# Prefix log-sum-exp along the sequence: later rows added in PSUM by VectorE in place of identity matmuls, and one drain of the chunk stream before the last tile

## Chip, cores and metric

One core of one Trainium2 chip. The metric is the device time of one execution in microseconds (us); a profiled execution has a span some 1.8 us below its time.

## The reference, cut to what matters

```python
B, S, D = (4, 4096, 4128)                     # x: float32, standard normal
out[:, 0, :] = x[:, 0, :]
for t in range(1, S):                          # running log-sum-exp over t
    out[:, t, :] = logaddexp(out[:, t - 1, :], x[:, t, :])
```

270.5 MB are read and 270.5 MB written.

## The kernel before

A tile holds up to 3 consecutive rows on each of 128 partitions, each row 4128 floats long: 6.34 MB. Each tile is worked off in four chunks of 1024 columns; the last chunk also carries a tail of 32 columns. ScalarE takes exp (as float16, written over the input), TensorE forms the prefix sum over the partitions into PSUM with triangular matrices, and ScalarE writes the logarithm of row 0. Row 1 is reached by adding its exps to PSUM with an identity matmul, then its logarithm is taken, then row 2. VectorE keeps the last partition's sum as a carry for the next tile.

```python
def stage(self, j):                            # row j of one chunk
    t, c, pt = self.t, self.c, self.pt
    nc.scalar.activation(t.xt[:, j, c * CH:(c + 1) * CH], pt, ACT.Ln)
    if j + 1 < t.r:
        for s in range(0, CH, MM):             # add row j + 1 by an identity matmul
            mm(pt[:, s:s + MM], ident, self.e(j + 1, s, s + MM), stop=j + 2 == t.r)
        if c == last and j == 0:               # the tail: 32 columns of all rows at once
            nc.scalar.activation(t.xt[:, :, t0:D], self.qt, ACT.Ln)
            keep(carry_t, self.qt[:, t.r - 1, :])
    else:
        keep(carry[c], pt)                     # two VectorE operations
...
chunks = [Chunk(s, c) for s in steps for c in range(n_main)]
for g in range(len(chunks) + R - 1):           # three chunks in flight, each one row apart
    for d in range(R - 1, -1, -1):
        if 0 <= g - d < len(chunks) and d < chunks[g - d].t.r:
            k = chunks[g - d]
            k.stage(d)
            if k.c == last and d + 1 == k.t.r:
                k.t.store()                    # then the load of the tile three ahead
                ...
    if g + 2 < len(chunks):
        chunks[g + 2].exp()
    if g + 1 < len(chunks):
        chunks[g + 1].head()
```

Four tile buffers, so three loads run ahead. Four of the 44 tiles have two rows: the first, and the last of the other three batches. T is the tile before the last, L the last. The matmuls with which a chunk begins are called its head below, and the two VectorE operations that save its carry its carry pair.

The softmax here doesn't subtract the row's maximum and nothing guards it: scores larger than these inputs give would overflow.

## Time and profile before

| | before |
|---|---|
| time, median | 1262.82 us |
| DMA | 541 MB, share 9 tenths or more in 39 of 40 slices |
| ScalarE / TensorE / VectorE busy | 75% / 55% / 36% |
| granted TensorE clock | 0.77 |

In a group line the number after the bar is busy time in us, then the mean in ns of one; after the second bar comes the idle time just before these instructions and what ended most of it.

### The profile page before, as it was taken

What the parts mean: (1) busy time and instruction counts of PE and PEld (TensorE: products, weight loads), DVE (VectorE), ACT (ScalarE), POOL (GpSimd) and SP (SyncE); (2) the same over time, 40 slices, a digit from 0 to 9 for tenths busy, and PEclk for the clock granted to TensorE, in tenths of its full rate; (3) what the DMA queues carried; (4) which work ended last, traced back from release to release, by engine and by line L of the source; (5) the groups of instructions that cost most, each with busy time, mean ns of one, the idle gap of its engine ahead of it and who ended that gap; (6) DMA issues with size and microseconds to landing.
All of it is one profiled execution on the core that took longest, in us unless ns stands there. A gap on an engine that the chain in (4) does not pass through costs nothing.

```text
span 1261.0 us, 6165 instructions
## 1 busy us (share of the span) xinstructions
PE 688.7 (55%) x2268; PEld 237.0 (19%) x2268; DVE 451.4 (36%) x445; ACT 947.3 (75%) x733; POOL 2.2 (0%) x13
## 2 busy tenths in 40 slices
PE   3665554555555555655346555555634755664552
PEld 1222111111121111211112211111211211221120
DVE  2443333333333333334424333333442433333344
ACT  5997777777777777778569777777966977777794
POOL 0000000000000000000000000000000000000000
PEclk9887777777677777777768777787777777778786
DMA  9999999999999999999999999999999999999998
GB/s 411 410 439 431 432 427 434 438 430 432 433 437 431 432 432 436 432 427 436 431 433 436 437 429 431 436 436 432 430 434 435 432 431 432 434 435 431 433 422 347
DMA packets 12702, 541.46 MB, mean 429 GB/s; under 512 B 1408, under 2 KB 1408, under 8 KB 1408
## 3 DMA queue, kind: packets, MB, share of 16 engines
q1 hardware_dynamic: 12672, 541.07, 99.4%
q8 instruction: 18, 0.29, 0.1%
q14 instruction: 12, 0.10, 0.0%
HBM read 270.53 MB, written 270.53 MB: 429 GB/s over the span
## 4 chain that ended last, share of the span: by engine, by line
DMA 69%; ACT 21%; PE 5%; issue 2%; DVE 1%; SPq 0%; ACTq 0%
DMA xt<-in_x_dram 67%; ACT xt L128 11%; ACT xt L162 10%; PE pt L88 5%; DMA out_dram<-xt 2%; ACT xt L167 0%; SPq L116 0%; DVE carry L92 0%; DVE carry L93 0%; ACTq L231 0%; SPq L113 0%; ACTq L128 0%; PE qt L88 0%
## 5 line engine op out<-in xcount | busy, mean ns | idle before, releaser
L128 ACT ACTIVATE xt<-xt 128x3072 f16<-128x3072 f32 (+3 forms) x176 | 478.5, 2719 | 247.9 <-DMA xt<-in_x_dram 247.8
L88 PE MATMUL pt<-xt,ident 128*128 128x512 f16 x672 | 251.3, 470 | 530.7 <-ACT xt L162 530.4
L162 ACT ACTIVATE xt<-pt 128x1024 f32<-128x1024 f32 x512 | 487.6, 1030 | 2.5 <-PE pt L88 0.7
L92 DVE CAST carry<-pt 32x1024 f16<-32x1024 f32 x176 | 216.4, 1230 | 761.0 <-ACT xt L162 760.7
L88 PE MATMUL pt<-xt,excl 128*128 128x512 f16 x672 | 247.0, 504 | 0.0
L93 DVE TENSOR_TENSOR carry<-pt,carry 32x1024 f16<-32x1024 f32 x176 | 215.9, 1227 | 6.1
L88 PEld LDWEIGHTS <-ident 128*128 128x128 f16 x672 | 70.1, 104 | 677.7 <-issue 654.0
L88 PE MATMUL pt<-xt,incl 128*128 128x512 f16 x352 | 152.0, 526 | 23.6 <-ACT xt L128 15.0
L88 PEld LDWEIGHTS <-excl 128*128 128x128 f16 x756 | 92.5, 124 | 141.0 <-issue 108.1
L88 PE MATMUL pt<-carry,pick 128*128 128x512 f16 x320 | 109.8, 429 | 0.0
L88 PEld LDWEIGHTS <-incl 128*128 128x128 f16 x480 | 45.2, 111 | 129.7 <-DVE carry L93 95.2
L88 PEld LDWEIGHTS <-pick 128*128 128x128 f16 x360 | 40.6, 113 | 57.0 <-issue 34.3
L167 ACT ACTIVATE xt<-qt 128x96 f32<-128x96 f32 (+1 forms) x44 | 10.9, 249 | 45.7 <-PE pt L88 45.7
L92 DVE CAST carry_t<-qt 32x32 f16<-32x32 f32 x44 | 8.7, 197 | 25.5 <-ACT xt L167 25.4
L88 PE MATMUL qt<-xt,incl 128*128 128x64 f16 (+2 forms) x128 | 12.3, 196 | 0.0
L88 PE MATMUL qt<-xt,excl 128*128 128x64 f16 (+1 forms) x84 | 10.6, 187 | 0.0
L93 DVE TENSOR_TENSOR carry_t<-qt,carry_t 32x32 f16<-32x32 f32 x44 | 8.5, 193 | 1.5
L88 PE MATMUL qt<-carry_t,pick 128*128 128x96 f16 (+1 forms) x40 | 8.2, 204 | 0.0
L83 DVE MEMSET carry<- 128x512 uint32 x4 | 1.9, 485 | 1.1 <-PEq L220 1.0
L70 ACT ACT_TABLE_LOAD x1 | 1.3, 1283 | 0.8 <-PEq L220 0.8
L35 POOL TENSOR_SCALAR_AFFINE_SELECT pick<-pick 128x128 f16<-128x128 f16 x2 | 0.6, 294 | 0.1
L25 POOL TENSOR_SCALAR_AFFINE_SELECT incl<-incl 128x128 f16<-128x128 f16 x1 | 0.3, 294 | 0.0
(11 smaller groups left out, 1.9 us busy)
## 6 DMA issues: line engine op xcount, KB each, us to landing
xt<-in_x_dram SPq DMA_DIRECT2D x40, 6192.0 KB, 42.2
out_dram<-xt SPq DMA_DIRECT2D x40, 6192.0 KB, 28.1
xt<-in_x_dram SPq DMA_DIRECT2D x4, 4128.0 KB, 37.3
out_dram<-xt SPq DMA_DIRECT2D x4, 4128.0 KB, 23.0
```

The costliest lines, as they stand in the source:

```text
L25: nc.gpsimd.affine_select(out=t, in_=t, pattern=[[1, P]], compare_op=mybir.AluOpType.is_ge, fill=0.0, base=base, channel_multiplier=-1,)
L35: nc.gpsimd.affine_select(out=t, in_=t, pattern=[[step, P]], compare_op=mybir.AluOpType.not_equal, fill=1.0, base=base, channel_multiplier=1,)
L70: nc.scalar.preload_act_table_set("natural_log_exp_and_others")
L83: nc.vector.memset(t, 0.0)
L88: nc.tensor.matmul(pt, lhsT=w, rhs=rhs, start=start, stop=stop, skip_group_check=True)
L92: nc.vector.tensor_copy(cr[HI:HI + 32, :], pt[HI:HI + 32])
L93: nc.vector.tensor_tensor(out=cr[LO:LO + 32, :], in0=pt[HI:HI + 32], in1=cr[HI:HI + 32, :], op=mybir.AluOpType.subtract,)
L128: nc.scalar.activation(self.t.half[:, :, 2 * c0:2 * c0 + w], self.t.xt[:, :, c0:c0 + w], ACT.Exp,)
L162: nc.scalar.activation(t.xt[:, j, c * CH:(c + 1) * CH], pt, ACT.Ln)
L167: nc.scalar.activation(t.xt[:, :, t0:D], self.qt, ACT.Ln)
```

## The change

The intent: take load off TensorE and use a VectorE that is idle two thirds of the time; and let the next to last tile's store go out without waiting for the last tile's exps. For that the stream of chunks is drained: all chunks of T are finished before L's first exp. The diff is shortened; lines with `...` or in brackets stand for what is left out.

```diff
     def stage(self, j):
         nc.scalar.activation(t.xt[:, j, c * CH:(c + 1) * CH], pt, ACT.Ln)
         if j + 1 < t.r:
-            for s in range(0, CH, MM):
-                mm(pt[:, s:s + MM], ident, self.e(j + 1, s, s + MM), stop=j + 2 == t.r)
+            add(pt, pt, self.e(j + 1, 0, CH))            # VectorE, in place in PSUM
             if c == last and j == 0:
                 nc.scalar.activation(t.xt[:, :, t0:D], self.qt, ACT.Ln)
     def tail_head(self):
+        e = [self.e(i, CH, CH + tail) for i in range(r)]
         for i in range(r):                               # before: all rows by broadcast matmuls
-            e = self.e(i, CH, CH + tail)
-            mm(qt[:, i:, :], incl, to(e, r - i), start=i == 0)
-            if i:
-                mm(qt[:, :i, :], excl, to(e, i))
+            mm(qt[:, 0, :], excl if i else incl, e[i], start=i == 0)
...
+        for i in range(1, r):
+            add(qt[:, i, :], qt[:, i - 1, :], e[i])
...
-    chunks = [Chunk(s, c) for s in steps for c in range(n_main)]
-    (one stream of chunks)
+    for part in (steps[:-1], steps[-1:]):                # the stream drains in between
+        chunks = [Chunk(s, c) for s in part for c in range(n_main)]
+        (the same loop)
```

More of the change, by code (lines that the diff above doesn't have):

```diff
@@ L29, in tri, with ones_at @@
         return t
-    def ones_where_zero(bases, step, name):
+    def ones_at(rows, name):
         t = pool.tile([P, P], FP16, name=name)
         nc.gpsimd.memset(t, 0.0)
-        for base in bases:
+        for row in rows:
             nc.gpsimd.affine_select(
-                out=t, in_=t, pattern=[[step, P]], compare_op=mybir.AluOpType.not_equal,
-                fill=1.0, base=base, channel_multiplier=1,
+                out=t, in_=t, pattern=[[0, P]], compare_op=mybir.AluOpType.not_equal,
+                fill=1.0, base=-row, channel_multiplier=1,
             )
@@ L43, in _constants @@
         tri(-1, "excl"),
-        ones_where_zero([0], -1, "ident"),
-        ones_where_zero([-(HI + 31), -(LO + 31)], 0, "pick"),
+        ones_at([HI + 31, LO + 31], "pick"),
     )
@@ L71 @@
     consts = ctx.enter_context(tc.tile_pool(name="consts", bufs=1))
-    incl, excl, ident, pick = _constants(nc, consts)
+    incl, excl, pick = _constants(nc, consts)
     bufs = 4
@@ L85, with mm, add @@
     ctx.enter_context(tc.manual_schedule())
-    def mm(pt, w, rhs, start=False, stop=False):
-        nc.tensor.matmul(pt, lhsT=w, rhs=rhs, start=start, stop=stop, skip_group_check=True)
+    def mm(pt, w, rhs, start=False):
+        nc.tensor.matmul(pt, lhsT=w, rhs=rhs, start=start, stop=False, skip_group_check=True)
+    def add(o, a, v):
+        nc.vector.tensor_tensor(out=o, in0=a, in1=v, op=mybir.AluOpType.add)
     def keep(cr, pt):
@@ L149, in tail_head @@
             qt = self.qt = full[:, :r, :]
-            to = lambda v, n: v.unsqueeze(1).to_broadcast([P, n, tail])
+            e = [self.e(i, CH, CH + tail) for i in range(r)]
             for i in range(r):
-                e = self.e(i, CH, CH + tail)
-                mm(qt[:, i:, :], incl, to(e, r - i), start=i == 0)
-                if i:
-                    mm(qt[:, :i, :], excl, to(e, i))
+                mm(qt[:, 0, :], excl if i else incl, e[i], start=i == 0)
             if not t.first:
-                mm(qt, pick, to(carry_t, r))
+                mm(qt[:, 0, :], pick, carry_t)
+            for i in range(1, r):
+                add(qt[:, i, :], qt[:, i - 1, :], e[i])
         def stage(self, j):
@@ L188 @@
     stored = 0
-    chunks[0].exp()
-    chunks[1].exp()
-    chunks[0].head()
-    for g in range(len(chunks) + R - 1):
-        for d in range(R - 1, -1, -1):
-            if 0 <= g - d < len(chunks) and d < chunks[g - d].t.r:
+    for part in (steps[:-1], steps[-1:]):
+        chunks = [Chunk(s, c) for s in part for c in range(n_main)]
+        chunks[0].exp()
+        chunks[1].exp()
+        chunks[0].head()
+        for g in range(len(chunks) + R - 1):
+            for d in range(R - 1, -1, -1):
+                if not (0 <= g - d < len(chunks) and d < chunks[g - d].t.r):
+                    continue
                 k = chunks[g - d]
@@ L201 @@
                     stored += 1
-        if g + 2 < len(chunks):
-            chunks[g + 2].exp()
-        if g + 1 < len(chunks):
-            chunks[g + 1].head()
+            if g + 2 < len(chunks):
+                chunks[g + 2].exp()
+            if g + 1 < len(chunks):
+                chunks[g + 1].head()
 _INS = ['x']
```

## The prediction

> **What bounds the kernel now.** I read the page's engine totals and its forty slices first, then the groups, then the SyncE queue's waits, and last the end of the run in two-microsecond windows and in order of time, because the first views say that only the ends can matter.
>
> ```profile
> span 1261.0 us, 6165 instructions
> ...
> PE 688.7 (55%) x2268; PEld 237.0 (19%) x2268; DVE 451.4 (36%) x445; ACT 947.3 (75%) x733; POOL 2.2 (0%) x13
> ...
> DMA  9999999999999999999999999999999999999998
> ...
> q1 hardware_dynamic: 12672, 541.07, 99.4%
> ...
> L88 PE MATMUL pt<-xt,ident 128*128 128x512 f16 x672 | 251.3, 470 | 530.7 <-ACT xt L162 530.4
> L162 ACT ACTIVATE xt<-pt 128x1024 f32<-128x1024 f32 x512 | 487.6, 1030 | 2.5 <-PE pt L88 0.7
> L92 DVE CAST carry<-pt 32x1024 f16<-32x1024 f32 x176 | 216.4, 1230 | 761.0 <-ACT xt L162 760.7
> ...
> L93 DVE TENSOR_TENSOR carry<-pt,carry 32x1024 f16<-32x1024 f32 x176 | 215.9, 1227 | 6.1
> ```
>
> No compute engine is above 75%, while the DMA engines are at 9 tenths or more in 39 of 40 slices. 541.07 MB at the 433 GB/s or so of the middle slices is 1250 us of the 1261. One full tile (three rows of 4128 floats on 128 partitions, 6.34 MB) takes 14.6 us each way, and the stores are indeed issued 29.3 us apart (1153.25, 1182.61, 1212.01 in the SyncE queue). ScalarE needs only about 21.9 us per tile: four times one exp (2.66 from start to start) and three Ln (0.92 each), 5.4 us per chunk, plus 0.25. It then waits for the next load, 247.8 us in all. So in the stream a compute change is hidden as long as a store is issued before the transfers in the queue run out. A store takes 28.1 us to land against 14.6 of its own, so at each issue the slowest DMA engine still holds some 13.5 us of older work. Only the start, where the queue is short, and the end, where nothing is left to overlap, can show the change.
>
> The end, as windows (the last three fields are PE clock, DMA share, GB/s):
>
> ```profile
> 1226.00:1228.00 2.00, 1.54 (x7) 0.60 (x7) 0.51 (x3) 1.89 (x2) 0.00 (x0) 1.00 0.80 347
> 1228.00:1230.00 2.00, 0.00 (x0) 0.00 (x0) 0.90 (x1) 2.00 (x4) 0.00 (x0) 1.00 0.63 272
> 1230.00:1232.00 2.00, 1.64 (x5) 0.55 (x5) 1.56 (x2) 2.00 (x2) 0.00 (x0) 0.65 0.23 99
> 1232.00:1234.00 2.00, 2.00 (x6) 0.70 (x5) 0.36 (x1) 2.00 (x3) 0.00 (x0) 0.50 0.10 33
> 1234.00:1236.00 2.00, 0.85 (x4) 0.13 (x2) 1.97 (x2) 2.00 (x3) 0.00 (x0) 0.99 0.93 396
> ```
>
> and the same stretch in order of time (start, length, engine):
>
> ```profile
> 1220.78 1.91 ACT L128 ACTIVATE xt<-xt 128x2048 f16<-128x2048 f32 x1 [1.34 <-DMA xt<-in_x_dram]
> ...
> 1233.63 10.83 SPq L116 DMA_DIRECT2D out_dram<-xt  x2
> ...
> 1243.09 1.02 ACT L162 ACTIVATE xt<-pt 128x1024 f32<-128x1024 f32 x1
> ```
>
> Call the tile before the last T (three rows) and the last one L (two rows, 4.23 MB). L's load lands at 1220.7. The queue then runs dry: the shares of the four windows from 1226 to 1234 fall 4.5 us short of full. T's store comes only at 1233.6, because ScalarE runs L's first three exps between T's last Ln's. From 1234 T's 6.34 and L's 4.23 MB flow without a gap until 1258.2, and the span ends 2.8 us later. L's store is issued at 1244.1, while T's transfer lasts until 1234.0 + 14.6 = 1248.6: L has 4.5 us of slack today.
>
> **What the Trainium skill says.** "VectorE: DVE Perf Modes", section "The perf-mode tier table", gives tensor_tensor with any PSUM operand only the 1x mode; its errata section has (N+151)/0.96 ns for an fp32 add, 1224 ns at N = 1024. The trace agrees: the subtraction with a PSUM input and 1024 columns took 1227 ns. Partitions should not matter, so I take 1.23 us for the new 128x1024 add, and 1.27 from start to start as between the two carry operations (1229.10, 1230.37). "PSUM — Partial Sum Buffer", section "The four PSUM rules", says that VectorE's writes leave the accumulation bits alone; here no matmul follows an add in its group, so the result is safe. "DMA: Bandwidth & Descriptors", section "Where 436 GB/s comes from", puts the ceiling at 435.2 GB/s; the 427 to 439 of the middle slices agree, so the stream has nothing to gain.
>
> **The change, part by part.**
> (1) Removed: 672 identity matmuls, 251.3 us of PE and 70.1 us of weight loads; none on the DMA path. PE goes to about 430 us.
> (2) Added on VectorE: 336 adds of 1.23 us, 413 us, and 84 tail adds at about 0.2 (as the 32-column rows take 0.19 to 0.20), 17 us: 451 + 430 = 881 us, 70%. Per chunk it now has two carry operations and two adds, 4 x 1.27 = 5.1 us, against ScalarE's 5.4. It fits, barely, and the tail adds can push it over by a microsecond once per tile. With some 13.5 us of work queued that costs nothing in the stream. Under load ScalarE's Ln's find their operand ready; the 1.1 us that the tail's Ln waits for an identity matmul queued behind it is gone, so stores come 0.6 to 1.3 us earlier. At the start, where tile 1's store (63.44) meets an almost empty queue, that may save 0.3 us.
> (3) The drain. All of T must now leave before L's first exp, and while no exps are in between, VectorE (5.1 us per round of four operations) and not ScalarE sets the pace, since each Ln of a chunk waits for an add that stands behind another chunk's carry pair. I lay out the instructions in the changed program's order with the durations above. (The same laying-out of the kernel before gives 1233.65 and 1244.2 for its last two stores, against 1233.63 and 1244.1 measured.)
>
> T's load landing at 1196.2 as before, T's fourth exp starts at 1212.6 (before: 1213.65). T0's third, T1's second and T2's first Ln run from 1215.4 to 1218.2. VectorE: carry T0 1216.4 to 1218.9, add T1 to 1220.2, add T2 to 1221.5, tail adds to 1221.9. ScalarE waits: T1's third Ln at 1220.2, T2's second at 1221.5, T3's first at 1222.4, the tail's at 1223.3. VectorE: carry T1 1221.9 to 1224.4, add T2 to 1225.7, add T3 to 1227.0, tail carry and carry T2 to 1230.0, add T3 to 1231.2. T3's third Ln ends at 1232.3: T's store goes out 1.3 us earlier than before, no more.
>
> L then starts at 1232.2, where before its first exp ran at 1220.8. Exps L0 and L1 to 1235.9, L0's first Ln 1235.8, exp L2 1236.7, L0's second Ln 1238.5, L1's first 1239.4, exp L3 1240.3. VectorE: carry L0 1239.6 to 1242.1, add L1 to 1243.3; L1's second Ln 1243.4, L2's first 1244.3; carry L1 to 1246.9, add L2 to 1248.2; L2's second Ln 1248.2, L3's first 1249.1; carry L2 1249.3 to 1251.8, add L3 to 1253.1; L3's second Ln ends at 1254.1. L's store goes out 10 us later than before.
>
> (4) Sum. T's transfer runs 1232.8 to 1247.4; then the DMA stands idle until L's store at 1254.1 + 0.5 = 1254.6, where before it began at 1248.6. The end moves by 6.0 us. With 0.3 saved at the start and some 0.4 for eight to ten hand-overs between VectorE and ScalarE that I took at 0.03 each: 1262.87 + 6.0 - 0.3 + 0.4 = 1269.0.
>
> **Rivals.**
> (a) The drain pays: T's store fills the hole that opens at 1226, and L keeps up. The 4.5 us short in the windows is the most that it can give: 1258.5. For it speaks the intent; against it L's 4.5 us slack, which an 11.4 us later start of its first exp uses up.
> (b) VectorE becomes the bound of the stream. It would take adds above 1.4 us (two carry operations of 1.27 and two of those exceed 5.4), and then ScalarE, at 5.4 x 4 = 21.9 us of 29.3, would still have over 7 us to give. Speaking for it only the start, 27 to 64 us, where ScalarE is busy 28.3 of 30 us and the queue short: 1 to 3 us more, 1271.
> (c) The matmul clock: at half clock (0.50 and 0.65 in the windows at 1230 to 1234) a head of L takes 2.8 us instead of 1.5. My schedule has few places where it shows, T3's head and L0's first; about 2.4 us more, 1271.4. Against: fewer matmuls should leave the clock high, and it is 1.00 in most windows of the end.
> (d) L's instructions overlap better than laid out, and all moves are hidden: 1263.
>
> **Range and chances.** The direction rests on one fact of order (L's exps behind T's last Ln) and on durations that are measured. (c) and slow hand-overs give the upper end, 1273; shorter drains and part of (a) the lower, 1263.5. A change of 2% is 25 us, and T's and L's drains together are not that long, so within 2% is nearly sure: 0.97. Slower by over 2% would need the stream itself to lose its DMA bound: 0.02. Faster by over 2% is below the transfer time of 541 MB: 0.01.
>
> **What would show it.** The new add at 1.2 to 1.25 us; VectorE near 880 us and PE near 430; stores in the stream still 29.3 us apart. At the end: T's store 1 to 2 us before 1233.6, ScalarE idle several times for 1 to 2 us on VectorE's adds, L's first exp directly after T's last Ln, L's store near 1254, the DMA share at zero for about 6 us around 1250, and the span near 1267. I am wrong if L's store comes before 1249, or if the store spacing in the stream changes.

## More of the kernel before

The page is shown in the prediction. One more group of it, which the prediction did not show, turned out to matter, the tail's Ln of the kernel before:

```profile
L167 ACT ACTIVATE xt<-qt 128x96 f32<-128x96 f32 (+1 forms) x44 | 10.9, 249 | 45.7 <-PE pt L88 45.7
```

44 short Ln's, one per tile, each found ScalarE waiting, 1.04 us on average, for an identity matmul into `pt`. The Ln reads `qt`, not `pt`.

## The result, and the profile after

The changed kernel takes 1281.99 us (median; 1281.17 to 1282.36) against 1262.82 before. Ratio 1.0151, 95% interval 1.0133 to 1.0168. It is slower by 1.5%. Predicted were 1269.0, with a range of 1263.5 to 1273.

The page of the changed kernel, the lines that answer to those in the prediction:

```profile
span 1280.6 us, 5200 instructions
...
PE 544.8 (43%) x1512; PEld 176.2 (14%) x1512; DVE 865.4 (68%) x865; ACT 950.6 (74%) x733; POOL 1.8 (0%) x11
...
DMA  9989999999999999999999999999999999999986
...
L160 ACT ACTIVATE xt<-pt 128x1024 f32<-128x1024 f32 x512 | 490.8, 1027 | 20.0 <-DVE pt L89 17.2
...
L89 DVE TENSOR_TENSOR pt<-pt,xt 128x1024 f32<-128x1024 f32 x336 | 398.1, 1228 | 26.9 <-ACT xt L160 21.5
...
L164 ACT ACTIVATE xt<-qt 128x96 f32<-128x96 f32 (+1 forms) x44 | 10.9, 248 | 145.2 <-DVE pt L89 145.2
```

The add takes 1228 ns, as predicted, and VectorE's busy time (865 us, 881 predicted) is right. But the third of the DMA slices is at 8 tenths, so the stream's start lost transfers, and the tail's Ln now waits 145.2 us, 3.3 per tile, where it waited 1.04.

What one such wait looks like in order of time in the changed kernel (start, length, engine; in square brackets the engine's idle time before and what ended it; TensorE rows left out):

```profile
577.42 2.83 ACT L160 ACTIVATE xt<-pt 128x1024 f32<-128x1024 f32 x3
578.45 1.23 DVE L93 CAST carry<-pt 32x1024 f16<-32x1024 f32 x1 [2.73 <-ACT xt L160]
579.72 1.23 DVE L94 TENSOR_TENSOR carry<-pt,carry 32x1024 f16<-32x1024 f32 x1
580.98 2.36 DVE L89 TENSOR_TENSOR pt<-pt,xt 128x1024 f32<-128x1024 f32 x2
...
583.37 0.25 ACT L164 ACTIVATE xt<-qt 128x96 f32<-128x96 f32 x1 [3.12 <-DVE pt L89]
583.52 2.75 ACT L129 ACTIVATE xt<-xt 128x3072 f16<-128x3072 f32 x1
```

ScalarE is done with its three Ln's at 580.25. It then stands still until 583.37, until VectorE has finished a carry pair and two chunk adds, though the tail's own two adds were done before (they ran at 575.29). Only then can the next exp start.

Where this costs transfers, the start, in windows of five microseconds (after the length: busy us of TensorE, its weight loads, VectorE, ScalarE and GpSimd; the last three fields are granted clock, DMA share and GB/s). Before:

```profile
60.00:65.00 5.00, 4.45 (x12) 1.38 (x12) 2.06 (x3) 5.00 (x4) 0.00 (x0) 0.67 0.82 357
65.00:70.00 5.00, 2.50 (x11) 0.90 (x11) 1.87 (x2) 4.97 (x5) 0.00 (x0) 1.00 1.09 466
```

After:

```profile
60.00:65.00 5.00, 1.67 (x4) 0.29 (x2) 1.51 (x4) 4.57 (x4) 0.00 (x0) 0.50 1.10 476
65.00:70.00 5.00, 3.09 (x8) 1.02 (x8) 4.43 (x5) 5.00 (x5) 0.00 (x0) 0.53 0.00 0
```

The second tile's store is issued at 69.66 instead of 63.44, the third's at 96.28 instead of 86.17, and for five microseconds nothing moves at all. After the fourth store, and away from the two-row tiles at the batch boundaries, stores are some 29.3 us apart as before.

The end of the changed kernel, in order of time:

```profile
1239.43 0.25 ACT L164 ACTIVATE xt<-qt 128x96 f32<-128x96 f32 x1 [4.46 <-DVE pt L89]
...
1244.47 1.02 ACT L160 ACTIVATE xt<-pt 128x1024 f32<-128x1024 f32 x1 [2.96 <-DVE pt L89]
1245.39 3.84 ACT L129 ACTIVATE xt<-xt 128x2048 f16<-128x2048 f32 x2
...
1267.67 1.02 ACT L160 ACTIVATE xt<-pt 128x1024 f32<-128x1024 f32 x1
```

and in windows:

```profile
1242.00:1244.00 2.00, 0.00 (x0) 0.00 (x0) 1.97 (x2) 0.00 (x0) 0.00 (x0) 0.50 0.00 0
...
1260.00:1262.00 2.00, 0.00 (x0) 0.00 (x0) 1.94 (x3) 0.00 (x0) 0.00 (x0) 0.50 0.00 0
```

T's last Ln runs at 1244.47 and L's first exp directly behind it; T's store goes out at 1245.5, L's at 1268.7, against 1233.6 and 1244.1 before. Between 1260 and 1268 VectorE works, ScalarE mostly waits for it and the DMA stands idle.

### The profile page after: what moved, and what is told of

Read it like the earlier page. It is cut to its first block, busy times and chain, and to the rows that moved or that the text cites. A ratio compares the mean times of both kernels' runs of the same rounds, so it can differ in the third digit from the quotient of the medians.

```text
span 1280.6 us, 5200 instructions
## 1 busy us (share of the span) xinstructions
PE 544.8 (43%) x1512; PEld 176.2 (14%) x1512; DVE 865.4 (68%) x865; ACT 950.6 (74%) x733; POOL 1.8 (0%) x11
## 4 chain that ended last, share of the span: by engine, by line
DMA 58%; ACT 18%; DVE 16%; PE 6%; issue 1%; ACTq 0%; SPq 0%
DMA xt<-in_x_dram 58%; ACT xt L129 12%; ACT xt L160 6%; PE pt L86 6%; DVE carry L93 5%; DVE carry L94 5%; DVE pt L89 5%; ACT xt L164 1%; DVE qt L89 0%; ACTq L232 0%; PE qt L86 0%; SPq L114 0%; SPq L117 0%; ACTq L129 0%; ACTq L160 0%
## 5 line engine op out<-in xcount | busy, mean ns | idle before, releaser
L86 PE MATMUL pt<-xt,incl 128*128 128x512 f16 x352 | 161.1, 555 | 714.1 <-DVE carry L94 527.4
L93 DVE CAST carry<-pt 32x1024 f16<-32x1024 f32 x176 | 216.4, 1230 | 314.3 <-ACT xt L160 314.0
L89 DVE TENSOR_TENSOR pt<-pt,xt 128x1024 f32<-128x1024 f32 x336 | 398.1, 1228 | 26.9 <-ACT xt L160 21.5
L86 PE MATMUL pt<-xt,excl 128*128 128x512 f16 x672 | 295.0, 585 | 0.0
L94 DVE TENSOR_TENSOR carry<-pt,carry 32x1024 f16<-32x1024 f32 x176 | 215.8, 1226 | 6.1
L86 PE MATMUL pt<-carry,pick 128*128 128x512 f16 x320 | 151.2, 570 | 0.0
L86 PEld LDWEIGHTS <-incl 128*128 128x128 f16 x396 | 31.3, 107 | 828.9 <-issue 821.1
L164 ACT ACTIVATE xt<-qt 128x96 f32<-128x96 f32 (+1 forms) x44 | 10.9, 248 | 145.2 <-DVE pt L89 145.2
L86 PEld LDWEIGHTS <-pick 128*128 128x128 f16 x360 | 48.8, 136 | 80.4 <-issue 74.1
L89 DVE TENSOR_TENSOR qt<-qt,xt 128x32 f32<-128x32 f32 x84 | 16.7, 198 | 42.0 <-PE qt L86 40.6
L86 PE MATMUL qt<-xt,incl 128*128 128x32 f16 x44 | 9.3, 212 | 0.0
L86 PE MATMUL qt<-xt,excl 128*128 128x32 f16 x84 | 9.1, 183 | 0.0
L86 PE MATMUL qt<-carry_t,pick 128*128 128x32 f16 x40 | 7.3, 183 | 0.0
```

The source lines that it names most:

```text
L86: nc.tensor.matmul(pt, lhsT=w, rhs=rhs, start=start, stop=False, skip_group_check=True)
L89: nc.vector.tensor_tensor(out=o, in0=a, in1=v, op=mybir.AluOpType.add)
L93: nc.vector.tensor_copy(cr[HI:HI + 32, :], pt[HI:HI + 32])
L94: nc.vector.tensor_tensor(out=cr[LO:LO + 32, :], in0=pt[HI:HI + 32], in1=cr[HI:HI + 32, :], op=mybir.AluOpType.subtract,)
```

## The experiments

Theory W: the tail's Ln is one instruction over all rows. Its 32 columns lie at the end of each row, so as one stretch of addresses it runs from the end of row 0 to the end of row 2, and all the exps that the chunk adds of rows 1 and 2 still read lie inside. It is therefore held for these adds, with which it shares no element. In the kernel before the same hold fell on identity matmuls, which were quick; now it falls on VectorE's adds, which queue behind a carry pair. Rival V: it is VectorE's load and the low matmul clock that slow every round. Rival D: it is the drain. Whether the hold is put into the program when it is built or made by the chip, no run here shows; the profile infers what released a wait from semaphore events.

### The hold taken away

```diff
-  nc.scalar.activation(t.xt[:, :, t0:D], self.qt, ACT.Ln)
+  for i in range(t.r):
+      nc.scalar.activation(t.xt[:, i, t0:D], self.qt[:, i, :], ACT.Ln)
```

> The changed kernel with the Ln of the 32 tail columns written row by row (three small Ln's in place of one over all rows), nothing else moved. Theory W (a held wait): the one Ln over all rows spans, as a stretch of addresses, the rows that VectorE's chunk adds still read, so it is held until the adds of the last two chunks are done; ScalarE idles 3.3 us per tile for it, which empties the transfer queue at the start and lengthens the end. W expects the wait of the tail's Ln to fall from 145 us to under 40, the second tile's store at 62 to 64 us (not 69.7), no window without transfers at 65 to 70, and 1269 to 1272 us, near what was first predicted. Rival V (VectorE's load and the low matmul clock slow every round, the wait is incidental): second store still after 67, 1278 to 1282. Rival D (the drain is nearly all of the loss): 1278 to 1282 too.

Measured: 1270.26 us, ratio 1.0058 (1.0043 to 1.0073). Correct result. The group and one round:

```profile
L165 ACT ACTIVATE xt<-qt 128x32 f32<-128x32 f32 x128 | 16.5, 217 | 0.0
```

```profile
1198.59 2.83 ACT L160 ACTIVATE xt<-pt 128x1024 f32<-128x1024 f32 x3
1199.62 1.23 DVE L93 CAST carry<-pt 32x1024 f16<-32x1024 f32 x1 [6.72 <-ACT xt L160]
...
1201.30 0.38 ACT L165 ACTIVATE xt<-qt 128x32 f32<-128x32 f32 x3
...
1202.15 2.36 DVE L89 TENSOR_TENSOR pt<-pt,xt 128x1024 f32<-128x1024 f32 x2
```

The three small Ln's run at 1201.30, before VectorE's two adds at 1202.15, and the result is correct, so there is no data they need from them. The wait is 0.0. The second store is back at 63.55 (before: 63.44) and the window from 65 to 70 us has a DMA share of 1.09. 11.7 us of the 19.2 are gone. W holds; V and D each expected 1278 or more.

### The Ln moved ahead of the last chunk's add

```diff
-  add(pt, pt, self.e(j + 1, 0, CH))
   if c == last and j == 0:
       nc.scalar.activation(t.xt[:, :, t0:D], self.qt, ACT.Ln)
       keep(carry_t, self.qt[:, t.r - 1, :])
+  add(pt, pt, self.e(j + 1, 0, CH))
```

> The changed kernel with the tail's Ln (still one over all rows) and its carry issued ahead of the last chunk's first add. W in its exact form: the Ln is then held only by the add of the chunk before, which VectorE finishes 1.27 us earlier, so the wait falls by 1.2 to 1.4 us per tile, from 145 to about 90 us, the second store comes near 67, and the time is 1276 to 1279, between the changed kernel and e1. If the wait were for the tail's own adds or matmuls (rival), nothing changes: 1281 to 1282. If only the last chunk's add held it, all of it goes: 1269 to 1272.

Measured: 1274.54 us, ratio 1.0093.

```profile
L163 ACT ACTIVATE xt<-qt 128x96 f32<-128x96 f32 (+1 forms) x44 | 10.9, 248 | 86.0 <-DVE pt L89 86.0
```

```profile
576.12 1.23 DVE L89 TENSOR_TENSOR pt<-pt,xt 128x1024 f32<-128x1024 f32 x1
...
577.39 0.25 ACT L163 ACTIVATE xt<-qt 128x96 f32<-128x96 f32 x1 [1.99 <-DVE pt L89]
...
578.11 1.23 DVE L89 TENSOR_TENSOR pt<-pt,xt 128x1024 f32<-128x1024 f32 x1
```

The wait fell from 145.2 to 86.0, 1.35 us per tile: about one add's length, not to zero. The Ln starts when the add of the chunk before ends; the last chunk's own add now comes after it, at 578.11. So the Ln is held by the add of the chunk before as well, which reads other columns. That is what a stretch of addresses predicts and what neither the tail's own data nor the last chunk alone does. The time fell by more than I expected (1276 to 1279), probably because only what exceeds the queue's reserve (the transfers still queued when a store is issued) is lost: T's load landed at 1196.74 in this run, against 1204.23 in the changed kernel and 1195.92 without the hold. With two microseconds per tile held instead of three, nearly all the lost transfers were back.

### Each part alone

Adds and the held Ln without the drain (`for part in (steps,):`):

> The changed kernel with one chunk stream over all tiles, so without the drain. W: the start loses as before (second store near 69.7); laid out by hand with the corrected wait, the last two stores come near 1247.5 and 1265, and the time is 1278 to 1279.5: the drain was worth only 2 to 3 us. D (the drain is nearly all of the loss): 1264 to 1267. V: 1277 to 1280.

Measured: 1276.2 us, ratio 1.0107. Second store at 69.64, as in the changed kernel. It is below the expected range, as T's load landed at 1201.6, not at the 1204.2 I laid out from; up to there both programs issue the same work, and why it landed earlier is not shown. Still, D is excluded: without the drain 13.4 of 19.2 us remain.

The drain alone, with identity matmuls kept (the changed loop over `steps[:-1], steps[-1:]` put into the kernel before):

> The kernel before, identity matmuls kept, with the drain at the last tile's boundary. W: the stream as before (second store 63.4, store before the last two at 1212); the second last store 3 to 6 us earlier than 1233.6 (1227.4 laid out at full matmul clock, 1230.7 at half), the last at 1244 to 1253 depending on that clock, time 1259 to 1268, best guess 1261. D: 1275 or more.

Measured: 1262.81 us, ratio 0.9998 (0.9984 to 1.0013). T's store went out at 1227.73, 5.9 us earlier than before, and it bought nothing:

```profile
1242.00:1244.00 2.00, 1.25 (x6) 0.58 (x6) 1.41 (x2) 1.32 (x2) 0.00 (x0) 1.00 0.69 297
1244.00:1246.00 2.00, 0.97 (x9) 0.47 (x7) 1.53 (x2) 1.43 (x2) 0.00 (x0) 1.00 0.29 124
1246.00:1248.00 2.00, 0.37 (x2) 0.00 (x0) 1.74 (x4) 1.14 (x2) 0.00 (x0) 1.00 0.12 50
1248.00:1250.00 2.00, 0.00 (x0) 0.00 (x0) 1.97 (x2) 0.00 (x0) 0.00 (x0) 0.63 1.22 520
```

The share fades over six microseconds and T's transfer ends only at 1248, about when it ended before by the prediction's working (1248.6). L's store, 3.4 us later than before, falls just into the end of that fade. Whether this later store or the slow end of T's transfer kept the time up, these windows can't tell; the landing times further below speak for the latter.

VectorE's adds alone (no hold, no drain):

> VectorE adds with the tail's Ln row by row, and one stream without the drain: what is left of the change is VectorE's adds alone. W: the stream is that of e1; the adds still delay the end, since each Ln of the last chunks waits for an add behind a carry pair. Laid out by hand: last two stores near 1234.0 and 1251.5 at either matmul clock, no transfer between 1249 and 1252, time 1265 to 1267 (3 to 4 us over before, 4 under e1). If the drain is harmless with adds: 1270. If the adds cost nothing once the wait is gone: 1263.

Measured: 1265.11 us, ratio 1.0019 (1.0005 to 1.0033). The last store is issued at 1250.7, and there is one window without transfers, 1248 to 1250. So 414 us more on VectorE (865.4 against 451.4) cost 2.3 us, all at the end (T's load landed at 1196.0, before: 1196.2).

These steps lead from one kernel to the other: adds 2.3 (before to adds alone), the drain on top of adds 5.2 (1265.1 to 1270.3), the hold 11.7 (1270.3 to 1282.0). They add up to 19.2 by construction, and the shares depend on the order: the drain costs 0.0 without the adds, 5.2 with them, and 5.8 with adds and hold (1276.2 to 1282.0).

### Where the hold costs

The tail row by row in the first three tiles only (`if t.index < 3:`), one Ln over all rows in the other 41:

> The changed kernel with the tail's Ln row by row in the first three tiles only; the other 41 keep the held Ln. If the held wait costs where the transfer queue is short (W: the stores of the changed kernel fall behind those of e1 by 8.8 us within the first four tiles and by 2 to 3 more over the rest), this recovers 8 to 9.5 us: second store at 62 to 64, stores 29.3 us apart afterwards, time 1272.5 to 1274.5. If each of the 44 waits costs its share evenly (12 us over 44), three of them are worth 0.8 us: 1281.

Measured: 1275.04 us, ratio 1.0099: three waits of 44 were worth 7.0 of 11.7 us. Somewhat less than I expected, because of the 11.4 us by which the changed kernel's third last store is behind that of the kernel without the hold, 3.1 are the wait itself between the landing of T's load and that store (17.9 us against 14.8), and only 8.3 are transfers lost earlier (T's landing at 1204.2 against 1195.9). Of these this run recovered 6.9; the rest fell at the batch boundaries, where tiles of two rows make the queue short.

The kernel before with nothing but the Ln row by row:

> The kernel before with nothing but the tail's Ln row by row: its own held wait (46 us in all, 1.1 per tile, on identity matmuls) goes. W: in the stream and at the end a wait that small is hidden behind the transfers; second store up to 1 us earlier, time 1262.0 to 1263.0. If ScalarE's waits counted one for one, 46 us less the 14 us for the extra Ln's: 1230.

Measured: 1263.87 us, ratio 1.0008 (0.9995 to 1.0021): the same, if anything slower.

```profile
L168 ACT ACTIVATE xt<-qt 128x32 f32<-128x32 f32 x128 | 16.6, 220 | 0.0
```

So the 46 us in the kernel before were the same hold. Its second store was at 62.77 instead of 63.44; in the stream that is hidden.

### The matmul clock

Two idle matmuls after each Ln into a scratch bank that nothing reads, on top of the first experiment:

```diff
+  for s in range(0, CH, MM):
+      mm(scratch, pick, self.e(j + 1, s, s + MM), start=True)
   add(pt, pt, self.e(j + 1, 0, CH))
```

> e1 with the removed matmuls put back as idle load: after each Ln two matmuls of 512 columns into a scratch bank that nothing reads (the tail's PSUM pool goes to one buffer to make room). Theory C (the granted matmul clock follows the matmul load): the clock rises from 0.64 to 0.73 or more, the heads at the end run near full speed, the last store comes 1 to 2.5 us earlier than in e1 (1256.5), and the time is 1268 to 1270. Rival: the clock does not follow the load and stays at 0.62 to 0.66; the extra matmuls then stand in front of the heads and the time is 1270 to 1273.

Measured: 1270.33 us, ratio 1.0061, against 1270.26 without them. The granted clock rose from 0.64 to 0.77, so here it follows the load. The rest of theory C missed: the time did not change. The last store came at 1256.4, against 1256.5 in the first experiment: TensorE does next to nothing from 1226 to 1236 in either kernel (0.9 and 0.8 us of 10), and the clock is at 0.50 when L's first matmuls start. In part the equal time may be a coincidence: T's load landed 1.4 us later (1197.34 against 1195.92), and T's store followed 35.9 us after it instead of 37.5. The second fits the faster clock; why the load landed later is not shown.

### Closing the hole before T's store

The kernel without hold and drain, with T stored chunk by chunk and L in two halves; and the kernel before (Ln row by row) with the same pieces:

```diff
+  if self.pieces and c % self.pieces == self.pieces - 1:     # 1 for T, 2 for L
+      a, b = (c + 1 - self.pieces) * CH, D if c == last else (c + 1) * CH
+      nc.sync.dma_start(out=self.dram(out)[:, :, a:b], in_=self.xt[:, :, a:b])
```

> e5 with the last two tiles stored in pieces: the one before the last chunk by chunk, the last in two halves. If the end is set by when stores are issued and by nothing else (W), the hole between 1226 and 1234 closes: pieces from 1217 on, the last half's store near 1251.5, 2.1 MB after it, span end near 1259.5, time 1260 to 1262, so faster than before in spite of 430 us more on VectorE. If pieces with runs of 4 KB move slower, or the computing sets the end, 1265 to 1268.

> The kernel before (identity matmuls, one stream) with the tail's Ln row by row and the same pieces. W: transfers without a hole up to the end, 4.5 us less than before at the end and up to 1 us less at the start: 1257.5 to 1259.5. If pieces do not help: 1262 to 1263.

Measured: 1263.93 us, ratio 1.0009 (0.9996 to 1.0021), and 1264.79 us, ratio 1.0016 (1.0004 to 1.0029). Both missed; neither beats the kernel before. The first gained 1.2 us on its own control (1265.11), the second nothing on its own (1263.87). In the second the hole is closed, and still nothing is gained:

```profile
1230.00:1232.00 2.00, 1.57 (x7) 0.44 (x7) 1.46 (x2) 2.00 (x2) 0.00 (x0) 1.00 0.87 357
...
1254.00:1256.00 2.00, 0.00 (x0) 0.00 (x0) 0.00 (x0) 0.00 (x0) 0.00 (x0) 0.50 0.63 266
1256.00:1258.00 2.00, 0.00 (x0) 0.00 (x0) 0.00 (x0) 0.00 (x0) 0.00 (x0) 0.50 0.21 87
```

The share between 1230 and 1232 is 0.87 (before: 0.23), but the end now fades from 0.79 at 1252 to 0.10 at 1258.

Together with the drain alone this says that the fade before T's store was not free time. No view splits the time by DMA engine, but the packed trace keeps sixteen landing times of each transfer (`landings` in trace.npz), one per engine as I read them. In the kernel before, those of the store ahead of T's run from 1228.05 to 1235.61: some were done up to 7.6 us before the last one. The last landing of T's store is at 1250.46 there and at 1250.51 with the drain alone, although it was issued 5.9 us earlier; L's last is at 1260.22 and 1260.27. The last landings of these three stores are 14.9 and 9.8 us apart in the kernel before, about what T's and L's transfers take by themselves (14.6 and 9.8). So the late end sets the time, and it had no hole to close. With the pieces and identity matmuls the last landing is at 1261.68; T's four pieces took 15.3 us by their first landings (1227.93 to 1243.19), where a whole tile takes 14.6 to 14.7 in the stream of the kernel before, so the shorter runs add some 0.6. The gap between a transfer's first and last landing grows along the kernel before, from 0.54 us at the first load to 7.10 at 1181.55. Why, and whether it is the same engine each time, is not shown: the landing times carry no engine's name.

No run pointed to a version that beats the kernel before.

## Why the prediction was wrong

- The direction, the bound and the stream: right. Stores stay some 29.3 us apart after the start, and VectorE at 68% does not bound it.
- Part (2), the cost of the adds: right, 1.228 us for 1.23. Part (1) has TensorE at about 430 us busy; it was 544.8, as with the granted clock at 0.64 the matmuls that stayed took longer (`excl` 585 ns, 504 before).
- Part (2), last sentences: this is the step that failed. The prediction says that "the 1.1 us that the tail's Ln waits for an identity matmul queued behind it is gone, so stores come 0.6 to 1.3 us earlier". I saw the wait in the trace of before and took it for an accident of queueing. It was a hold, it was not removed but moved to VectorE, and it grew from 1.04 to 3.3 us per tile, because there the adds stand behind a carry pair. It was worth 11.7 us instead of minus 0.3. The first experiment shows it, the second shows which instructions hold. None of the signs that the prediction named for being wrong looks at this wait.
- That the start, where the queue is short, is where a wait shows: right as a place, with the wrong sign. Three tiles were worth 7.0 us.
- Part (3) and (4), the drain: right in mechanism, 1.3 us too small. Without the hold the measured loss is 7.4 us for the 6.1 predicted; T's store came at 1233.4 (1232.3 laid out) and L's at 1256.5 (1254.1). L's head took 2.7 us at half clock in that run (1235.23 to 1237.95), as rival (c) has it, where 1.5 was laid out; that this is the whole rest is argued.
- Rival (c) argued that fewer matmuls should leave the clock high. The opposite is so: 0.77 before, 0.64 after, 0.77 again with spare matmuls. The Trainium skill says as much, in "TensorE: Matmul & The Clock Gate", section "What's actually happening": the clock gate opens with recent activity. I did not look there.
- Rival (a), at most 4.5 us to gain from the hole before T's store: the reading of the windows was wrong. The drain alone sent T's store out 5.9 us earlier, its last landing came at the same time, and nothing was gained.

## What to carry to other kernels

When work is moved from one engine to another, waits that ended on the old work can move with it, also those that no data asks for. So for each small wait in the profile ask what the waiting instruction has in common with what released it; if it is nothing but a stretch of addresses, split the access (here worth 11.7 us in the changed kernel, and nothing in the kernel before). And where transfers bound a kernel, count a compute wait not by its sum (145 us here) but where the transfer queue is short: three tiles at the start were worth more than the other 41.

## What the Trainium skill lacked or had wrong

- None of its pages that I read tells of waits between instructions that touch no common element because one access, seen as a stretch of addresses, encloses the other. It would belong to "Perfetto Trace Analysis", section "Identifying Dependency Chains". Here it held ScalarE 145.2 us (3.3 per tile); with the access split by rows 0.0, result correct.
- "VectorE: DVE Perf Modes", section "The TRN2 errata": (N+151)/0.96, given for an fp32 add, also holds for an add in place in PSUM with one float16 operand from SBUF: 1224 ns by the formula, 1228 measured.
- "TensorE: Matmul & The Clock Gate", section "What's actually happening", agrees. The mean granted clock fell from 0.77 to 0.64 when the 672 identity matmuls and 84 small ones went, and rose to 0.77 with 672 idle ones. The mean alone says little: L's head, behind some ten idle microseconds, still ran at 0.50 and the time stayed at 1270.3.
- "DMA: Bandwidth & Descriptors", section "Latency and other measured facts", calls two of the sixteen engines usually slower, puts that down, as a guess, to transfers whose descriptors software writes, and gives no size. Here the transfers run on a hardware queue (q1 hardware_dynamic), and the sixteen landings of one transfer lie 0.5 us apart at the first load and 7.1 us apart at 1181 us; a store issued 5.9 us earlier ended no earlier (1250.51 against 1250.46).
